# Both feed-forwards: sixteen hidden tiles down by seven half products, two conditioning vectors by TensorE in attention, x added in the later groups

## The chip, the cores and the metric

One core of one Trainium2 chip (trn2). The metric is the device time of one execution in microseconds; the time of a kernel is the median over its runs. The program is written out flat: every instruction is placed once, in a fixed order on each engine, and all loads and stores are issued from one queue, SyncE's, in order.

## The reference, cut to what matters

One trunk layer with two feed-forwards around a token mixer. Context (128 tokens) and latent (1024 tokens) go through the same weights with conditioning vectors of their own. D is 1024, the hidden width of a feed-forward 2816, all in fp32.

```python
def modulate(x, g, shift, scale):
    return rmsnorm(x, g) * (1.0 + scale) + shift

def swiglu(h, w1, w3, w2):
    return (jax.nn.silu(h @ w1) * (h @ w3)) @ w2

def trunk_layer(x, mod, cache, lb, norm_g, ffn1, ffn2, mixer_w):
    m = [mod[:, i][:, None, :] for i in range(N_MOD)]
    x = x + 0.5 * m[2] * swiglu(modulate(x, norm_g[0], m[0], m[1]), *ffn1)
    mix, ctx = token_mixer(modulate(x, norm_g[1], m[3], m[4]), cache, lb, *mixer_w)
    x = x + m[5] * mix
    x = x + 0.5 * m[8] * swiglu(modulate(x, norm_g[2], m[6], m[7]), *ffn2)
    return x, ctx
...
        mod_p = (jax.nn.silu(c_ctx) @ w_ada[l] + b_ada[l]).reshape(1, N_MOD, D_MODEL)
        mod_s = (jax.nn.silu(c) @ w_ada[l] + b_ada[l]).reshape(c.shape[0], N_MOD, D_MODEL)
```

## The kernel before, in words

**Layout.** All 1152 tokens are worked on together, with the features on the partitions: x is eight tiles (KT) of 128 features by 1152 tokens, the hidden layer 22 tiles. Each fp32 operand is split into a high and a low half in fp32r, and a product takes three matmuls: high by high, high by low, low by high. ScalarE makes the high half by a cast, VectorE or GpSimd the low half by a subtraction.

**Stages on TensorE, in order:** the start (conditioning vectors 0 and 1, first norm); the first feed-forward's hidden half (to about 552 us of the profile); its down projection (to 834); the mixer's recurrence and its projections (to about 1560); attention, eight heads with eight steps t of 128 queries each; merge and output projection; the second feed-forward's hidden half (2200 to 2593); its down projection; the final norm.

**Hidden half (`ffn_fast`).** The first PLAIN tiles (4 in the first feed-forward, 3 in the second) are plain products. The others are made by seven half products each: a Strassen-like scheme over two halves of the inner dimension and two of the tokens. The tokens are cut into four quarters of 288, paired (3, 0) and (1, 2). One line, L1746, does these matmuls, with weights from `fast_ops` (cast L1720, low half L1721). Up to six weights are prepared ahead.

**Down projection, the plain form.** `down_group` takes two hidden tiles at a time and forms their product with w2 for eight rows of x and three chunks of 384 tokens: matmuls L473, L474, L475, three per product. VectorE then adds product times gate to x (L502). The first feed-forward did all 22 tiles this way, the last pair and the next norm in `down_last`.

**Down projection, the product form.** The second feed-forward did 16 of its tiles in eight pairs: `down_fast` walks three GROUPS, (first tile, number of pairs) = (3, 2), (7, 3), (13, 3), and in each group four sweeps (m = 0 to 3). A sweep makes the two rows m and m + 4 of x by seven products in the order 1, 6, 7, 5, 2, 4, 3, each for two pairs of quarters (`down_sweep`, L1939, 288 columns). Its parts:

- `pair_sums` (L1783 to L1786, VectorE) forms sums of two hidden tiles in the hidden half; they go to `xd` in DRAM.
- `down_xs` loads them again (`xr`, L1899) and splits them: cast on ScalarE (L1909), low half (L1910) on VectorE for the second pair of a group, else on GpSimd. The next group's are split in the last sweep of a group.
- `pair_weights` (L1807 to L1810, GpSimd) forms the sums of w2 for the first two groups in the hidden half: 5 pairs by 4 m = 20 pieces, stored as `wsum`. The last group's sums are formed on the spot (L1878, GpSimd) in `down_ops`, which also splits all weights (L1883 ScalarE, L1884 VectorE), one product at a time.
- VectorE folds the results: product times gate into x (L1926, in up to two segments where latent and context tokens meet), and products 1 and 6 into a sum `su` (L1942 ScalarE, L1944 VectorE).
- x itself is loaded (`load_x`) under the last hidden tile, two rows at a time (L2056), before the first group.

**Conditioning vectors.** There are nine, m = 0 to 8. `ada_pe` makes 0 and 1 at the start on TensorE: the weights' rows stream against silu(c) of 32 columns, four matmuls side by side on the columns of the array (L263), then a copy and two transposes. `ada_sum` makes the others on VectorE, by products with an accumulated sum (L318): 2 to 5 in the first feed-forward's hidden half, 6 and 7 under its down projection (as `bg`), 8 in the second's hidden half.

**Buffers that matter.** 27 tiles "tt" of 128 x 1152, eight "wide", half and quarter sizes ("half", "hf"); PSUM banks up (3), dn (3), st, ps1 for the feed-forwards and mx (2) among those of attention. A load is issued only when its tile has come free.

## Time and profile before

| | us |
|---|---|
| median of 3 runs (2877.96 to 2881.16) | 2878.12 |
| profiled execution, its own time | 2878.52 |
| its span | 2876.7 |
| TensorE busy in it | 2780.8 |
| start, 0 to 148: TensorE busy | 123.67 of 148 |
| first hidden half, 148 to 552 | 402.37 of 404 |
| first down projection, 552 to 840 | 282.17 of 288 |
| recurrence and projections, 840 to 1560 | 702.28 of 720 |
| attention, 1560 to 1890 | 321.11 of 330 |
| merge, output, next norm, 1890 to 2200 | 293.85 of 310 |
| second hidden half, 2200 to 2593 | 393.00 of 393 |
| its three groups, 2593 to 2784 | 181.72 of 191 |
| last tiles and final norm, 2784 to 2877 | 80.62 of 93 |

The mean granted clock is 0.99. "Busy" is the time in which at least one instruction of an engine ran; matmuls overlap each other, so the pace of a stage is read from its length and its count of matmuls, and not from the mean duration of one (L1939: mean 297 ns). A bracket behind a timeline row, such as `[2.08 <-DVE x L1926]`, is the idle time before it and what ended it.

### The profile page before, as it was taken

What the parts mean: (1) busy time and instruction counts of PE and PEld (TensorE: products, weight loads), DVE (VectorE), ACT (ScalarE), POOL (GpSimd) and SP (SyncE); (2) the same over time, 40 slices, a digit from 0 to 9 for tenths busy, and PEclk for the clock granted to TensorE, in tenths of its full rate; (3) what the DMA queues carried; (4) which work ended last, traced back from release to release, by engine and by line L of the source; (5) the groups of instructions that cost most, each with busy time, mean ns of one, the idle gap of its engine ahead of it and who ended that gap; (6) DMA issues with size and microseconds to landing.
All of it is one profiled execution on the core that took longest, in us unless ns stands there. A gap on an engine that the chain in (4) does not pass through costs nothing. (4 is left out here: it accounts for less than half of the span.)

```text
span 2876.7 us, 55574 instructions
## 1 busy us (share of the span) xinstructions
PE 2780.8 (97%) x21138; PEld 2642.9 (92%) x21138; DVE 2023.5 (70%) x4433; ACT 1324.6 (46%) x2714; POOL 962.9 (33%) x997
## 2 busy tenths in 40 slices
PE   6999999999999999999999999989999999999998
PEld 5999999999999999988998778779989999999997
DVE  7687777577778777877356777756665666568775
ACT  6433323321166676766535787730552322234332
POOL 0132232354222122222144454442442443323450
PEclk9999999999999999999999999999999999999999
DMA  6643333663121111112512001262553443358421
GB/s 238 212 146 124 126 123 115 225 208 109 62 81 55 50 57 37 57 47 68 173 56 75 18 17 30 76 217 91 181 159 108 146 158 127 100 164 264 131 88 66
DMA packets 215147, 329.59 MB, mean 115 GB/s; under 512 B 23712, under 2 KB 138976, under 8 KB 214880
## 3 DMA queue, kind: packets, MB, share of 16 engines
q1 hardware_dynamic: 214880, 326.04, 34.7%
q8 instruction: 167, 2.74, 0.4%
q14 instruction: 100, 0.82, 0.1%
HBM read 243.56 MB, written 82.40 MB: 113 GB/s over the span
## 5 line engine op out<-in xcount | busy, mean ns | idle before, releaser
L1746 PE MATMUL b<-xo,wo 128*128 128x288 f32 x3552 | 482.0, 295 | 0.0
L1746 PEld LDWEIGHTS b<-xo,wo 128*128 128x128 f32 x3552 | 474.3, 188 | 0.0
L1746 PE MATMUL b<-bh,wo 128*128 128x288 f32 x1776 | 365.1, 295 | 1.6 <-ACT et L1756 1.6
L473 PE MATMUL mm<-xh,wh 128*128 128x384 f32 (+1 forms) x1008 | 352.3, 350 | 10.2 <-DVE sg L750 5.6
L474 PE MATMUL mm<-xl,wh 128*128 128x384 f32 (+1 forms) x1008 | 342.4, 340 | 0.0
L475 PE MATMUL mm<-xh,wl 128*128 128x384 f32 (+1 forms) x1008 | 341.9, 339 | 0.0
L1746 PEld LDWEIGHTS b<-bh,wo 128*128 128x128 f32 x1776 | 288.6, 188 | 1.9 <-ACT et L1756 1.8
L502 DVE SCALAR_TENSOR_TENSOR x<-dn,modt,x 128x256 f32<-128x256 f32 (+4 forms) x472 | 225.7, 499 | 87.8 <-PE dn L475 86.5
L1746 PE MATMUL b<-bl,wo 128*128 128x288 f32 x888 | 261.4, 294 | 0.0
L473 PEld LDWEIGHTS mm<-xh,wh 128*128 128x128 f32 (+1 forms) x1008 | 190.0, 188 | 19.9 <-DVE sg L750 7.4
L1720 ACT CAST wo<-raw 128x512 fp32r<-128x512 f32 x185 | 114.8, 621 | 183.7 <-issue 79.5
L474 PEld LDWEIGHTS mm<-xl,wh 128*128 128x128 f32 (+1 forms) x1008 | 189.7, 188 | 2.3 <-issue 0.7
L1939 PE MATMUL d<-xd,wd 128*128 128x288 f32 x1344 | 182.0, 297 | 9.3 <-DVE x L1926 7.8
L475 PEld LDWEIGHTS mm<-xh,wl 128*128 128x128 f32 (+1 forms) x1008 | 189.6, 188 | 1.0
L1939 PEld LDWEIGHTS d<-xd,wd 128*128 128x128 f32 x1344 | 180.1, 190 | 11.1 <-ACT xd L1909 4.0
L1721 DVE TENSOR_TENSOR wo<-raw,wo 128x512 fp32r<-128x512 f32 x185 | 127.8, 692 | 66.6 <-ACT wo L1720 64.2
L318 DVE SCALAR_TENSOR_TENSOR junk<-wada,cb 128x512 bf16<-128x512 f32 x224 | 163.3, 729 | 12.8 <-DMA wada<-in_w_aT 11.9
L1461 POOL TENSOR_TENSOR ehl<-e,ehl 128x512 fp32r<-128x512 f32 x93 | 121.5, 1311 | 142.4 <-ACT ehl L1459 80.6
L1746 PEld LDWEIGHTS b<-bl,wo 128*128 128x128 f32 x888 | 167.0, 188 | 0.0
L247 POOL TENSOR_TENSOR wl<-raw,wh 128x1024 fp32r<-128x1024 f32 (+3 forms) x51 | 101.8, 1996 | 170.3 <-ACT wh L246 113.2
L1721 DVE TENSOR_TENSOR wo<-ws,wo 128x512 fp32r<-128x512 f32 x74 | 71.6, 967 | 112.4 <-ACT wo L1720 112.2
L1720 ACT CAST wo<-ws 128x512 fp32r<-128x512 f32 x74 | 45.6, 617 | 223.2 <-POOL ws L1716 223.1
(438 smaller groups left out, 7176.1 us busy)
## 6 DMA issues: line engine op xcount, KB each, us to landing
raw<-in_w SPq DMA_DIRECT2D x148, 256.0 KB, 3.4
wada<-in_w_aT SPq DMA_DIRECT2D x112, 256.0 KB, 3.2
raw<-in_w SPq DMA_DIRECT2D x42, 512.0 KB, 3.7
raw<-in_w_in SPq DMA_DIRECT2D x41, 512.0 KB, 3.4
xr<-xd SPq DMA_DIRECT2D x56, 288.0 KB, 4.2
hr<-hs SPq DMA_DIRECT2D x26, 576.0 KB, 5.8
hb<-hd SPq DMA_DIRECT2D x44, 288.0 KB, 3.4
hs<-et SPq DMA_DIRECT2D x84, 144.0 KB, 2.2
```

Source lines behind the costliest of these rows:

```text
L247: pin((eng or self.nc.gpsimd).tensor_sub(wl, raw, wh))
L318: nc.vector.scalar_tensor_tensor(junk, ws[n % 2], 1.0, cs[s], ALU.mult, ALU.mult, accum_out=o)
L473: pin(nc.tensor.matmul(ps, wh, xh, start=start and i == 0, stop=False))
L474: pin(nc.tensor.matmul(ps, wh, xl, start=False, stop=False))
L475: pin(nc.tensor.matmul(ps, wl, xh, start=False, stop=stop and i == n - 1))
L502: nc.vector.scalar_tensor_tensor(self.x[m][:, a:b], ps[:, a - lo : b - lo], self.modt[:, gm, m, s : s + 1], self.x[m][:, a:b], ALU.mult, A ...
L1461: eng.tensor_sub(el, e, eh)
L1720: nc.scalar.copy(wh, src[i])
L1721: nc.vector.tensor_sub(wl, src[i], wh)
L1746: nc.tensor.matmul(ps, w[:, k], x[:, k, :QW], start=first, stop=last, skip_group_check=home != i)
L1939: nc.tensor.matmul(ps, w[:, k], xv, start=start, stop=stop, skip_group_check=home != i)
```

## The change

Both feed-forwards now take sixteen hidden tiles, the ones right behind the plain tiles, down by the seven half products, in groups of 2, 3 and 3 pairs; the six others stay plain. `pair_sums` and `pair_weights` run in both hidden halves. `pair_weights` also stores the sums for the last group's m = 0, so there are 5 x 4 + 3 = 23 pieces.

x isn't loaded before the groups. In group 0 the first product to reach a piece of x writes it as product times gate, VectorE for products 7 and 3, ScalarE for 2 and 4. In groups 1 and 2 each sweep loads one row of the old x and adds it after the sweep's fourth product, in two VectorE operations of 576 columns.

Vectors 6 and 7 are made in attention by `ada_fill`: from the second head on, in steps t = 3 and 7, it alternates between loading two rows of weights and eight matmuls on them (four column groups by two rows), with the partial sums added on VectorE and two transposes at the end. The mixer's constants are made in parts during group 1.

```diff
-GROUPS = (3, 2), (7, 3), (13, 3)
+GROUPS = (0, 2), (4, 3), (10, 3)
+PAIRED = 16
...
+    def ada_fill(self):
+
+        nc, a = self.nc, self.a
+        for m in (6, 7):
+            acc = self.fp.tile([P, 256], F32, tag="ada", bufs=1, name="adar")
+            for k in range(0, KT, 2):
+                w = [self.tt(F32, "wada")[:, :D] for _ in range(2)]
+                for i in range(2):
+                    nc.sync.dma_start(w[i], a["w_ada"][(k + i) * P : (k + i + 1) * P, m * D : (m + 1) * D])
+                yield
+                ps = self.pp.tile([P, 256], F32, tag="mx", bufs=2, name="adap")
+                for i in range(2):
+                    for g in range(4):
+                        v = slice(32 * g, 32 * g + 32)
+                        nc.tensor.matmul(
+                            ps[v, :],
+                            self.sc[:, k + i, :],
+                            w[i][:, 256 * g : 256 * g + 256],
...
+                if k:
+                    nc.vector.tensor_add(acc, ps, acc)
+                else:
+                    nc.vector.tensor_copy(acc, ps)
+                yield
+            self.ada_turn(m, acc, "mx", 2)
+            yield
...
+                    if h and t in (3, 7):
+                        next(fill, None)
...
-            for m in range(KT // 2):
+            for m in range(KT // 2 if j < n - GROUPS[-1][1] else 1):
...
-            own = g == len(GROUPS) - 1
+            own = g == len(GROUPS) - 1 and m > 0
...
-        def add(mi, q, src):
+        def add(mi, q, src, new=None):
             for lo, hi, s in segs(QUARTERS[q]):
                 xv, v = self.x[mi][:, lo:hi], slice(lo - q * QW, hi - q * QW)
+                if first and new:
+                    if new == "act":
+                        nc.scalar.activation(xv, src[:, v], AF.Identity, scale=self.modt[:, gm, mi, s : s + 1])
+                    else:
+                        nc.vector.tensor_scalar(xv, src[:, v], self.modt[:, gm, mi, s : s + 1], None, ALU.mult)
+                    continue
                 nc.vector.scalar_tensor_tensor(xv, src[:, v], self.modt[:, gm, mi, s : s + 1], xv, ALU.mult, ALU.add)
...
+                if g:
+                    xa.append((4 * g - 4 + m, load_x(4 * g - 4 + m)))
 
                 def after():
                     nonlocal k
+                    if xa and k == 3:
+                        i, t = xa.pop()
+                        for v in range(2):
+                            c = ts(v, 2 * QW)
+                            self.nc.vector.tensor_add(self.x[i][:, c], t[:, c], self.x[i][:, c])
...
-                if n != 3:
+                if n != (3 if l else 6):
                     next(sums, None)
...
-                        self.x[k] = load_x(k)
-                elif f == NF - 1:
...
+                        self.x[k] = self.tt(F32, f"x{k}")
...
-            self.bg = self.ada_sum((6, 7), lambda: self.bank("up", "cb", D // 2), partial(self.tt, F32), self.slim)
...
+        self.down_fast(w2, X, xg, dops, dmade, load_x, load_h, split_h, gm, nxt)
```

TensorE where the first feed-forward goes from its hidden half to its down projection. `b` is a hidden product, `dn` a plain one of the down projection, `d` a half product of it; `hh` and `hl` are the halves of a hidden tile. Before:

```order
L1746 MATMUL b_6131<-bh,wo 128x288
L473 MATMUL dn<-hh,wh 128x384
L474 MATMUL dn<-hl,wh 128x384
L475 MATMUL dn<-hh,wl 128x384
L473 MATMUL dn<-hh,wxh 128x384
L474 MATMUL dn<-hl,wxh 128x384
L475 MATMUL dn<-hh,wxl 128x384
```

And now, at the same place:

```order
L1787 MATMUL b_6545<-bh,wo 128x288
L1987 MATMUL d_6699<-xd,wd 128x288 x6
L1987 MATMUL d_6707<-xd,wd 128x288 x6
L1987 MATMUL d_6720<-xd,wd 128x288 x6
L1987 MATMUL d_6728<-xd,wd 128x288 x6
L1987 MATMUL d_6747<-xd,wd 128x288 x6
L1987 MATMUL d_6755<-xd,wd 128x288 x6
L1987 MATMUL d_6766<-xd,wd 128x288 x6
L1987 MATMUL d_6774<-xd,wd 128x288 x6
```

The pair of plain tiles that stood first is gone; at once the eight products of the first sweep come, each of six matmuls of 288 columns.

TensorE in the second head of attention, at step t = 7 (`mtr` are transposes of row maxima, `po` the products with the values, `sps` the scores that come next). Before:

```order
L475 MATMUL qps<-qnh_17389,wl 128x384
L1418 MATMUL mtr<-ident,m_18845 1x128 x4
L1428 MATMUL po<-ehl,V 128x512
L1429 MATMUL po<-ehl,V 128x512
L1430 MATMUL po<-ehl,V 128x512
L1452 MATMUL sps<-qh_17836,kth_17721 128x512
L1453 MATMUL sps<-qh_17836,ktl_17722 128x512
L1454 MATMUL sps<-ql_17837,kth_17721 128x512
```

And now:

```order
L511 MATMUL qps<-qnh_18197,wl 128x384
L1459 MATMUL mtr<-ident,m_19658 1x128 x4
L1469 MATMUL po<-ehl,V 128x512
L1470 MATMUL po<-ehl,V 128x512
L1471 MATMUL po<-ehl,V 128x512
L306 MATMUL adap<-wada,sc 32x256 x8
L1493 MATMUL sps<-qh_18644,kth_18529 128x512
L1494 MATMUL sps<-qh_18644,ktl_18530 128x512
L1495 MATMUL sps<-ql_18645,kth_18529 128x512
```

Eight matmuls of vector 6 (`adap`) stand between the last `po` and the first `sps`.

VectorE in the second feed-forward's group 0, third sweep, which makes rows 2 and 6 of x (`d7`, `d5` and so on are PSUM banks of the products, `modt` the gate, `wd` a weight's low half, `xd` that of a sum of hidden tiles). Before:

```order
L1926 SCALAR_TENSOR_TENSOR x6_30109<-d7_30500,modt_92,x6_30109 128x288
L1926 SCALAR_TENSOR_TENSOR x6_30109<-d7_30508,modt_92,x6_30109 128x288
L1884 TENSOR_TENSOR wd_30516<-raw_30338,wd_30516 128x256
L1926 SCALAR_TENSOR_TENSOR x6_30109<-d5_30519,modt_92,x6_30109 128x288
L1926 SCALAR_TENSOR_TENSOR x6_30109<-d5_30527,modt_92,x6_30109 128x288
L1884 TENSOR_TENSOR wd_30535<-raw_30338,wd_30535 128x256
L1926 SCALAR_TENSOR_TENSOR x2_30107<-d1_30452,modt_92,x2_30107 128x160
L1926 SCALAR_TENSOR_TENSOR x2_30107<-d1_30452,modt_92,x2_30107 128x128
L1926 SCALAR_TENSOR_TENSOR x2_30107<-d1_30460,modt_92,x2_30107 128x288
L1884 TENSOR_TENSOR wd_30553<-wq_30405,wd_30553 128x256
```

And now:

```order
L1972 TENSOR_SCALAR x6_31071<-d7_31459,modt_92 128x288
L1972 TENSOR_SCALAR x6_31071<-d7_31467,modt_92 128x288
L1926 TENSOR_TENSOR wd_31475<-raw_31297,wd_31475 128x256
L1974 SCALAR_TENSOR_TENSOR x6_31071<-d5_31478,modt_92,x6_31071 128x288
L1974 SCALAR_TENSOR_TENSOR x6_31071<-d5_31486,modt_92,x6_31071 128x288
L1926 TENSOR_TENSOR wd_31494<-raw_31297,wd_31494 128x256
L1926 TENSOR_TENSOR wd_31512<-wq_31364,wd_31512 128x256
L1952 TENSOR_TENSOR xd_31578<-xr_31403,xd_31578 128x576
L1972 TENSOR_SCALAR x2_31070<-d5_31478,modt_92 128x288
```

Products 7 now write x without reading it, and the additions into `x2` that came from product 2 (`d1`) have left this queue. The additions of the old x stand in the sweeps of the next groups; in group 1's first sweep:

```order
L1974 SCALAR_TENSOR_TENSOR x4_30837<-d7_31850,modt_92,x4_30837 128x288
L1974 SCALAR_TENSOR_TENSOR x4_30837<-d7_31861,modt_92,x4_30837 128x288
L1926 TENSOR_TENSOR wd_31872<-raw_31604,wd_31872 128x384
L1974 SCALAR_TENSOR_TENSOR x4_30837<-d5_31875,modt_92,x4_30837 128x288
L2035 TENSOR_TENSOR x0_30836<-x0_31788,x0_30836 128x576
L1974 SCALAR_TENSOR_TENSOR x4_30837<-d5_31886,modt_92,x4_30837 128x288
L1926 TENSOR_TENSOR wd_31897<-raw_31604,wd_31897 128x384
L2035 TENSOR_TENSOR x0_30836<-x0_31788,x0_30836 128x576
```

Two operations of 576 columns take the loaded row `x0` into the row of x, between the folds of products 7 and 5 and the weights' low halves.

102 lines of the change are left out of this document (44 added, 58 removed).

## The prediction

> **What bounds the kernel now.** I read the head of the page first, then the busy time of each engine by stage, then what TensorE waited for, and last the timeline around its longest waits.
>
> ```profile
> span 2876.7 us, 55574 instructions
> PE 2780.8 (97%) x21138; PEld 2642.9 (92%) x21138; DVE 2023.5 (70%) x4433; ACT 1324.6 (46%) x2714; POOL 962.9 (33%) x997
> PEclk9999999999999999999999999999999999999999
> ```
>
> TensorE is busy 97% of the span and the clock row of the page stands at 9 throughout, so a change is worth what it does to TensorE's stream of matmuls, and work of another engine counts only where it makes that stream stop.
>
> ```profile
> core 0: us, PE busy (x) PEld busy (x) DVE busy (x) ACT busy (x) POOL busy (x), PEclk, DMA share, GB/s
> 560.00:780.00 220.00, 220.00 (x1255) 219.99 (x1254) 171.51 (x414) 41.13 (x40) 96.25 (x39) 1.00 0.42 143
> 2200.00:2593.00 393.00, 393.00 (x2975) 392.98 (x2974) 252.97 (x501) 117.32 (x243) 146.24 (x210) 1.00 0.44 142
> 2593.00:2784.00 191.00, 181.72 (x1346) 179.90 (x1345) 157.11 (x308) 77.15 (x144) 82.73 (x54) 0.99 0.54 170
> ...
> 148.00:552.00 404.00, 402.37 (x3038) 402.15 (x3037) 290.61 (x648) 126.91 (x246) 128.91 (x146) 1.00 0.41 131
> ```
>
> The rows give the pace of a matmul where nothing stops it. Between 560 and 780 us, in the first feed-forward's down projection, 1255 matmuls of 384 columns fill 220.00 us: 0.1753 us each. Between 2200 and 2593, 2975 matmuls of 288 columns fill 393.00 us: 0.1321 each. The second feed-forward's three groups of products (2593 to 2784) hold 1344 matmuls of 288 columns, which at that pace take 177.5 us; they took 191.0. So **13.5 us** of stalls lie there, and they are the best witness for what the first feed-forward will look like. The last row is the first feed-forward before its down projection, where VectorE is busy 290.61 of 404 us.
>
> ```profile
> 1600.00:1800.00 200.00, 198.28 (x954) 159.53 (x954) 148.53 (x280) 155.34 (x298) 96.97 (x82) 1.00 0.08 21
> ```
>
> In attention's middle heads TensorE is busy 198.28 of 200 us: what is added to its stream there is paid in full.
>
> **Part 1, the first feed-forward's down projection.** Sixteen tiles leave the plain form: 16 tiles x 8 rows x 3 chunks x 3 matmuls = 1152 of 384 columns, 1152 x 0.1753 = 201.9 us. In come 4 rows x 7 products x 2 pairs of quarters x 8 pairs of tiles x 3 = 1344 of 288 columns, 1344 x 0.1321 = 177.5 us. Without stalls that is **-24.4 us**. The six tiles left plain cost the same in both.
>
> ```profile
> PE dn L475 <- POOL wl L247: 1.0, 1, 1.0
> PE dn L473 <- DVE x L502: 0.4, 1, 0.4
> ```
>
> These two waits are all that the plain form lost in this stretch, 1.4 us, both where tiles change over; such change-overs stay, so I keep them. What comes in is the stall of the product form, S, which I take from the second feed-forward.
>
> ```profile
> 2637.40 3.60 PE L1939 MATMUL d<-xd,wd 128*128 128x288 f32 x24 [2.08 <-DVE x L1926]
> 2644.78 1.61 PE L1939 MATMUL d<-xd,wd 128*128 128x288 f32 x9 [3.79 <-DVE x L1926]
> ...
> 2724.38 2.63 PE L1939 MATMUL d<-xd,wd 128*128 128x288 f32 x18 [1.44 <-DVE su L1944]
> ...
> 2718.82 3.15 POOL L1910 TENSOR_TENSOR xd<-xr,xd 128x576 fp32r<-128x576 f32 x2
> 2721.93 1.52 POOL L1878 TENSOR_TENSOR wr<-wr,ws 128x384 f32<-128x384 f32 x1
> ...
> 2645.90:2649.30 3.40, 3.40 (x16) 3.40 (x15) 3.40 (x6) 1.80 (x3) 2.86 (x2) 0.50 0.84 254
> ```
>
> The first two rows are the change from group 0 to group 1: TensorE stood 2.08 and 3.79 us until VectorE had folded earlier products. Right behind it the granted clock was 0.50 for 3.4 us (16 matmuls where the next 3.4 us hold twice as many), which costs 1.7 us: 7.6 us in all. The third is in the first sweep of the last group: 1.44 us, and there GpSimd worked a weight sum (L1878) between two splits of `xd` (L1910), so the weight came late. The rest of the 13.5 us are stops under 1 us each.
>
> **Part 2, what the change does to S,** in both feed-forwards alike.
>
> ```profile
> L1926 DVE SCALAR_TENSOR_TENSOR x<-d,modt,x 128x288 f32<-128x288 f32 x114 | 56.3, 510 | 14.0 <-PE d L1939 12.9
> L1910 DVE TENSOR_TENSOR xd<-xr,xd 128x576 fp32r<-128x576 f32 x16 | 18.6, 1165 | 3.8 <-ACT xd L1909 3.7
> L1926 DVE SCALAR_TENSOR_TENSOR x<-d,modt,x 128x160 f32<-128x160 f32 x28 | 10.5, 377 | 1.4 <-PE d L1939 0.7
> L1926 DVE SCALAR_TENSOR_TENSOR x<-d,modt,x 128x128 f32<-128x128 f32 x28 | 9.5, 340 | 0.0
> ...
> L1942 ACT COPY su<-d 128x288 f32<-128x288 f32 x8 | 3.0, 400 | 1.3 <-PE d L1939 1.3
> ...
> 2593.00:2637.90 44.90, 42.45 (x318) 41.86 (x316) 35.71 (x79) 21.27 (x50) 11.71 (x8) 1.00 0.81 265
> 2637.90:2714.00 76.10, 72.31 (x533) 71.97 (x532) 61.43 (x108) 29.18 (x54) 31.95 (x22) 0.98 0.51 151
> 2714.00:2784.00 70.00, 66.96 (x500) 66.07 (x499) 59.97 (x123) 26.70 (x43) 39.07 (x26) 1.00 0.41 129
> ...
> SPq L1848 <- DMA x<-xs: 2.4, 1, 2.4
> SPq L1840 <- DMA x<-xs: 2.1, 2, 1.1
> SPq L1637 <- DMA x<-xs: 2.1, 2, 1.1
> SPq L1853 <- DMA x<-xs: 0.7, 1, 0.7
> ```
>
> (a) The last group's first sweep takes stored sums, so four GpSimd operations and their four waits on loads go: I take 2.5 us of stalls out, the 1.44 us above and about as much of the small ones near it; at least 0, at most 4. Its price, three more pairs' first sums, is made in the hidden half before (part 4).
> (b) In group 0, products 2 and 4 are written by ScalarE: per sweep six pieces of 288, 160 and 128 columns, twice 510 + 377 + 340 = 2.45 us, 9.8 us in four sweeps, leave VectorE, which was busy 35.71 of 44.90 us there. ScalarE, at 21.27 of 44.90, gets them; its nearest row, a copy of 288 columns from PSUM, took 0.400 us, so about 9 us: it stays below 31 of 45, but its queue also holds the weight and `xd` casts on which the change of group hangs. VectorE's remaining writes in group 0 lose their second operand. No row shows a `tensor_scalar` of this shape; between half of 510 ns and 510 ns, I take 510 by the nearest row, the addition it replaces.
> A sentence on the page "VectorE: DVE Perf Modes" of the Trainium skill, under "Why PSUM operands drop a tier", bears on this: an fp32 operand in PSUM keeps VectorE at one element per cycle, so dropping the second operand buys nothing. By it those 16 writes per feed-forward of about 0.5 us stay as dear; without it they would save some 4 us of VectorE's time in group 0, none of it on TensorE by itself. No run here shows it yet.
> (c) SyncE waited 2.4 + 2.1 + 2.1 + 0.7 = 7.3 us for loads of `x` just as group 0 began, with the loads of `xd` queued behind. Those loads move into groups 1 and 2, one per sweep, so group 1's `xd` can start earlier. With (b) I take 2 us off the 7.6 us of the change of group; bounds: 2 us more (ScalarE's longer queue) and 6 us less.
> (d) The adds come back later as 16 operations of 576 columns on VectorE per feed-forward. The row for such a size is L1910's, 1.165 us in the mean: 16 x 1.165 = 18.6 us onto groups 1 and 2, where VectorE is busy 61.43 of 76.10 and 59.97 of 70.00 us. That leaves 6 us of 146: the mean load fits, the bursts at the end of group 1, where `xd` splits stand in the same queue, do not. Behind each add stand the fold of a product (its PSUM bank) and the next weight's low half. I charge 1 us at the change from group 1 to 2 and 0.25 in each of the eight sweeps: 3 us; bounds 0 and 12.
> (e) The load's own wait. An add comes after four products of its sweep, 4 x 18 x 0.1321 = 9.5 us after it starts.
>
> ```profile
> x<-xs SPq DMA_DIRECT2D x8, 576.0 KB, 7.6
> ```
>
> A load of `x` took 7.6 us where eight went out together; singly I expect it in time, cost 0, and price the other case below.
>
> So S = 13.5 - 2.5 - 2 + 3 = 12, less what VectorE gains when GpSimd's sums no longer run beside it in one sweep; I take **S = 10 to 12, 10.5**. First feed-forward: -24.4 + 10.5 = -13.9. Second: 10.5 - 13.5 = **-3.0**.
>
> **Part 3, attention.** 16 rows of weights, each four matmuls of 32 columns of the array, enter TensorE's queue in eight pieces of eight; then two transposes per vector.
>
> ```profile
> 51.77 0.29 PE L475 MATMUL ps<-bh,wl 128*128 128x288 f32 x1
> 51.99 1.07 PE L263 MATMUL adap<-wada,sc 128*32 128x256 f32 x16
> 52.99 0.40 PE L473 MATMUL ps<-bh,wh 128*128 128x288 f32 x1
> 53.23 0.29 PE L474 MATMUL ps<-bl,wh 128*128 128x288 f32 x1
> ...
> 1629.22 0.39 PE L1428 MATMUL po<-ehl,V 128*128 128x512 f32 x1
> 1629.45 0.60 PE L1418 MATMUL mtr<-ident,m 128*1 128x128 f32 x4
> 1629.80 0.47 PE L1429 MATMUL po<-ehl,V 128*128 128x512 f32 x1
> 1630.12 0.39 PE L1430 MATMUL po<-ehl,V 128*128 128x512 f32 x1
> ```
>
> The first rows are the same piece where it stands now, in the start: sixteen records (two passes of each matmul), 1.07 us. Without it the matmul at 53.23 would follow that at 51.77 after two paces, at 52.03; so a piece costs 1.20 us, eight cost 9.6. Four transposes between `po` matmuls (1629.22 to 1630.12, 0.90 us where two paces of 0.23 would be 0.46) cost 0.44 us, so the new four cost 0.4 to 0.6. Sum **+10.1 us**, hidden by nothing, since TensorE stood 1.7 us in those 200. Bounds: 8 (some falls into stops of the later heads) and 13 (waits on a load or a PSUM bank shared with the row maxima). The 64 products on VectorE that it replaces (L318 under the first feed-forward's groups) lay beside a full TensorE, so their removal is worth 0 by itself.
> By the Trainium skill, "TensorE: Matmul & The Clock Gate", Part 3 on packing, column tiles overlap within a pass and a pass lasts one matmul plus about 4 ns per further tile: four passes of 0.39 us make about 1.6 us a piece, 12.5 us in all and a total some 3 us higher (an estimate from that page). The rows above overlap the passes too (1.07 us), and I go by the rows.
>
> **Part 4, the first feed-forward's hidden half.** It now makes pair sums and weight sums.
>
> ```profile
> L1786 DVE TENSOR_TENSOR hp<-et 128x288 f32<-128x288 f32 x16 | 7.3, 455 | 0.3
> ...
> L1810 POOL TENSOR_TENSOR wq<-wq 128x128 f32<-128x128 f32 x17 | 11.2, 656 | 0.0
> ```
>
> Pair sums: 64 operations x 0.455 = 29.1 us on VectorE, 290.61 + 29.1 = 320 of 404 us. Weight sums: 23 pieces x 4 x about 0.63 = 58 us on GpSimd, at 128.91 of 404. The second feed-forward carries both with VectorE at 252.97 of 393 and no stop of TensorE. Here VectorE has the vectors' products besides. Weights are cast up to six products ahead, so a burst has some 3.2 us per product (24 x 0.1321) to drain: I take 0.6 us; bounds 0 and 12.
>
> **The sum.** -24.4 + 10.5 + 0.6 - 3.0 + 10.1 = **-6.2 us**. The profiled execution had a span of 2876.7 and a time of 2878.5, 1.8 outside; the median of the runs is 2878.1. From the median: 2871.9, rounded to **2872**. Own range with S from 7 to 14 and attention from 8 to 12: first -16.8 to -9.8, second -6.5 to +0.5, attention +8 to +12: 2863 to 2881.
>
> **Rivals.**
> *The product form runs clean.* With SyncE free of `x` and GpSimd of four sums, the change of group passes without a stop over 1 us and without the half clock: S = 4 each. -20.4 - 9.5 + 10.1 + 0.6 = -19.2: 2859. For it: the second feed-forward's hidden half runs the same splits with no stop. Against: ahead of group 1 stand 14 splits on GpSimd of about 1.6 us (two took 3.15 above), against a sweep of 84 matmuls, 11 us.
> *VectorE fills up in groups 1 and 2.* A third of the 18.6 us shows, S = 16 to 17: -8.0 + 3.0 + 10.1 + 0.6 = +5.7: 2884. For it: 6 us of slack in 146. Against: the stops of a microsecond and more sit at the changes of group, and within the sweeps a VectorE busy 61.43 of 76.10 us costs little.
> *A late `x` holds VectorE (slower).* Place: the first add of a sweep, at the head of VectorE's queue, waiting for a transfer which SyncE issues only when a tile comes free and earlier loads in its queue have gone. It decides from the point where the load is issued 2 us after its sweep began (9.5 - 7.6). If half of the 16 are 3 us late, 24 us are added: -6.2 + 24 = +18: 2896. Against: one load per sweep has the transfer engines at a share of 0.51 and 0.41.
> *The first feed-forward's hidden half stops.* Eight pairs whose sums (8 x 0.455 = 3.6 us, more than a product's 3.2) hold the next eviction 1.5 us: +12: 2884.
> That the change does not do what it says I leave out: the new order shows all of it.
>
> **How the numbers follow.** Forecast 0.50 (of it 0.36 beyond -0.2%, 0.14 within); clean 0.16, faster; VectorE full 0.16 (0.08 within, 0.08 slower); late `x` 0.10, slower; hidden half 0.08 (0.05 within, 0.03 slower). 0.2% is 5.8 us, about what a measurement of this kernel tells from no change. Together: faster 0.52, same 0.27, slower 0.21. The range leaves out most of late `x` and the far end of clean: 2858 to 2886.
>
> **What would show it.** Right: in the first feed-forward's groups 1344 matmuls in 185 to 192 us; a stop of some microseconds at the change from group 0 to 1 in both, and none from the weight sums in the last group's first sweep; eight pieces of about 1.1 us in attention. Wrong: TensorE waiting for an `x` that waits for a transfer; stops before the down projection; attention longer by under 6 or over 14 us; or groups without stops.

## The result, and the profile after

The changed kernel is slower: 2901.11 us median of 6 runs (2896.81 to 2905.77) against 2878.04 (2874.03 to 2882.57, 6 runs), a ratio of 1.0075, interval 1.0063 to 1.0086. Forecast were 2872 us and a range of 2858 to 2886. The head of its page (span, busy times):

```profile
span 2899.6 us, 57126 instructions
PE 2773.9 (96%) x21462; PEld 2625.6 (91%) x21462; DVE 2064.7 (71%) x4420; ACT 1372.4 (47%) x2876; POOL 1013.4 (35%) x1114
```

TensorE has less to do (2773.9 us where it was 2780.8) and stands longer (126 where it was 96). The next view is the table by stretches, which I cut at the first and last matmul of a stage. Of the changed kernel: first hidden half, first groups, the six plain tiles, second groups.

```profile
core 0: us, PE busy (x) PEld busy (x) DVE busy (x) ACT busy (x) POOL busy (x), PEclk, DMA share, GB/s
151.20:580.20 429.00, 409.47 (x3025) 406.80 (x3024) 320.84 (x715) 119.77 (x256) 179.09 (x238) 0.98 0.55 169
580.30:769.30 189.00, 182.12 (x1345) 179.93 (x1344) 162.17 (x308) 81.00 (x165) 75.26 (x48) 0.99 0.57 173
769.40:846.50 77.10, 77.10 (x437) 76.57 (x436) 51.18 (x105) 34.37 (x62) 27.22 (x18) 1.00 0.30 107
2616.70:2807.10 190.40, 180.99 (x1347) 178.50 (x1346) 163.65 (x306) 82.43 (x166) 75.17 (x49) 1.00 0.58 181
```

And the first hidden half of the kernel before, cut in the same way:

```profile
150.20:552.50 402.30, 400.67 (x3025) 400.45 (x3024) 289.08 (x646) 125.64 (x244) 126.71 (x144) 1.00 0.41 132
```

The first hidden half is the news. For the same 3025 matmuls TensorE stood 19.5 us where it had stood 1.6, and was busy 8.8 us longer, at a mean clock of 0.98: slow matmuls behind the stops. VectorE's and GpSimd's busy time don't show it, 320.84 and 179.09 of 429. By such cuts the two profiled executions (spans 2876.7 and 2899.6) differ so:

| stage, us | before | after | difference | forecast |
|---|---|---|---|---|
| first hidden half | 402.3 | 429.0 | +26.7 | +0.6 |
| first down projection (groups 189.1, rest 77.2) | 281.4 | 266.3 | -15.1 | -13.9 |
| attention, first score to last value product | 326.3 | 333.5 | +7.2 | +10.1 |
| second hidden half | 422.0 | 424.1 | +2.1 | 0 |
| second groups | 191.1 | 190.4 | -0.7 | -3.0 |
| all else | 1253.6 | 1256.3 | +2.7 | 0 |
| sum | 2876.7 | 2899.6 | +22.9 | -6.2 |

One line is off by far more than the rest together. What waited for what in that half (engine and line, what it waited for, total us, times, longest):

```profile
PE b L1787 <- ACT et L1797: 11.8, 8, 2.9
PE b L1787 <- DVE et L1795: 7.7, 3, 3.3
...
ACT wo L1761 <- POOL ws L1757: 143.2, 17, 14.3
...
DVE junk L354 <- DMA wada<-in_w_aT: 38.2, 12, 5.9
...
POOL wq L1849 <- DMA wq<-in_w: 103.7, 18, 12.6
...
SPq L1854 <- POOL wq L1851: 43.5, 17, 4.4
```

TensorE's 11 waits are for folds: product 2's on ScalarE, product 5's on VectorE. In the same stretch ScalarE stood 143.2 us with its casts for GpSimd's sums of the hidden weights (`ws`), VectorE 38.2 for the vectors' weights, GpSimd 103.7 for the loads of the weight sums, SyncE 43.5 in front of their stores. Such totals don't say which wait held a fold. The timeline around the longest stop does (SyncE's issues, then GpSimd, ScalarE, VectorE, TensorE):

```profile
327.04 0.81 SPq L1846 DMA_DIRECT2D wq<-in_w  x2
331.82 0.33 SPq L1854 DMA_DIRECT2D wsum<-wq  x1
332.69 0.33 SPq L1855 DMA_DIRECT2D wsum<-wq  x1
333.07 0.91 SPq L1739 DMA_DIRECT2D raw<-in_w  x2
334.08 0.38 SPq L335 DMA_DIRECT2D wada<-in_w_aT  x1
...
329.44 0.97 POOL L1849 TENSOR_TENSOR wq<-wq 128x128 f32<-128x128 f32 x1 [2.34 <-DMA wq<-in_w]
331.34 0.46 POOL L1851 TENSOR_TENSOR wq<-wq 128x128 f32<-128x128 f32 x1
331.76 0.91 POOL L1852 TENSOR_TENSOR wq<-wq 128x128 f32<-128x128 f32 x1
336.65 1.43 POOL L1757 TENSOR_TENSOR ws<-raw 128x256 f32<-128x256 f32 x2 [3.98 <-DMA raw<-in_w]
338.04 1.41 POOL L1757 TENSOR_TENSOR ws<-ws,raw 128x256 f32<-128x256 f32 x2
...
339.48 0.62 ACT L1761 CAST wo<-ws 128x512 fp32r<-128x512 f32 x1 [9.60 <-POOL ws L1757]
...
334.11 0.45 DVE L1793 TENSOR_TENSOR et<-b,et 128x288 f32<-128x288 f32 x1
338.89 1.11 DVE L354 SCALAR_TENSOR_TENSOR junk<-wada,cb 128x512 bf16<-128x512 f32 x1 [4.33 <-DMA wada<-in_w_aT]
340.13 1.00 DVE L1762 TENSOR_TENSOR wo<-ws,wo 128x512 fp32r<-128x512 f32 x1
341.06 0.45 DVE L1795 TENSOR_TENSOR et<-b,et 128x288 f32<-128x288 f32 x1
...
335.04 3.34 PE L1787 MATMUL b<-xo,wo 128*128 128x288 f32 x24
341.65 0.37 PE L1787 MATMUL b<-bh,wo 128*128 128x288 f32 x1 [3.27 <-DVE et L1795]
```

Read it backwards. TensorE stood 3.27 us for VectorE's L1795 (341.06). Two operations stand ahead of it in VectorE's queue: the vectors' product L354, which VectorE reached at 334.56 and could not start for 4.33 us, since its weights (`wada`) were issued at 334.08 only, and L1762, the low half of a hidden weight. L354 was through at 340.00. L1762 needs ScalarE's cast of the same weight, which ended at 340.10; it started at 340.13. So the cast is what held the fold: with `wada` there in time, L1762 could have started only 0.03 us earlier. The cast had waited 9.60 us for GpSimd's sum `ws` (L1757), and GpSimd 3.98 us for its load, `raw`. SyncE issued `raw` at 333.07, because it stood from 327.85 to 331.82 in front of L1854, the store of a weight sum that GpSimd was still forming (L1851 ended at 331.80, L1852 at 332.67); `wada` stood there too. GpSimd in turn was late because its own loads, issued at 327.04, had just come. So in this stop it is one loop through one queue: a store that waits for an engine makes every load behind it late, those of the engine itself among them.

All eleven stops end in this way: the fold comes right behind the cast or the low half of a `ws` weight that was late. TensorE never waited for the weight itself, which is prepared several products ahead of its use; the fold stood behind it in the queue. In ten of the eleven GpSimd had just stood for `raw` (0.65 to 6.09 us). In six, 14.6 of the 19.5 us, `raw` was the next load behind the stores of a weight sum. The longest stop on ScalarE:

```profile
435.46 0.62 ACT L1761 CAST wo<-ws 128x512 fp32r<-128x512 f32 x1 [9.30 <-POOL ws L1757]
...
437.35 0.70 ACT L1797 ACTIVATE et<-b 128x288 f32<-128x288 f32 x2
...
437.85 0.37 PE L1787 MATMUL b<-bh,wo 128*128 128x288 f32 x1 [2.94 <-ACT et L1797]
```

The Trainium skill, "PSUM — Partial Sum Buffer", section "Engine vs sequencer instructions", says that the queues of ScalarE, VectorE and GpSimd are strictly first in, first out. The trace agrees: the folds L1795 and L1797 came only after operations on weights that they have nothing to do with, and that were late by the casts' waits of 9.60 and 9.30 us.

### The profile page after: what moved, and what is told of

It reads as the page before. It is cut to its first block, busy times and chain, and to the rows that moved or that the text cites. A ratio compares the mean times of both kernels' runs of the same rounds, so it can differ in the third digit from the quotient of the medians.

```text
span 2899.6 us, 57126 instructions
## 1 busy us (share of the span) xinstructions
PE 2773.9 (96%) x21462; PEld 2625.6 (91%) x21462; DVE 2064.7 (71%) x4420; ACT 1372.4 (47%) x2876; POOL 1013.4 (35%) x1114
## 5 line engine op out<-in xcount | busy, mean ns | idle before, releaser
L1787 PE MATMUL b<-bh,wo 128*128 128x288 f32 x1776 | 373.3, 299 | 19.5 <-ACT et L1797 11.8
L1987 PE MATMUL d<-xd,wd 128*128 128x288 f32 x2688 | 363.5, 296 | 16.3 <-DVE x L1974 14.3
L1987 PEld LDWEIGHTS d<-xd,wd 128*128 128x128 f32 x2688 | 358.6, 189 | 21.0 <-ACT wd L1925 10.2
L509 PE MATMUL mm<-xh,wh 128*128 128x384 f32 (+1 forms) x1008 | 351.8, 349 | 11.4 <-DVE sg L788 5.7
L509 PEld LDWEIGHTS mm<-xh,wh 128*128 128x128 f32 (+1 forms) x1008 | 189.1, 188 | 21.3 <-DVE sg L788 7.5
L510 PEld LDWEIGHTS mm<-xl,wh 128*128 128x128 f32 (+1 forms) x1008 | 189.3, 188 | 2.3 <-issue 0.7
L511 PEld LDWEIGHTS mm<-xh,wl 128*128 128x128 f32 (+1 forms) x1008 | 189.0, 187 | 0.9
L1952 POOL TENSOR_TENSOR xd<-xr,xd 128x576 fp32r<-128x576 f32 x70 | 118.4, 1717 | 173.5 <-ACT xd L1951 129.1
L1762 DVE TENSOR_TENSOR wo<-raw,wo 128x512 fp32r<-128x512 f32 x185 | 129.7, 702 | 37.8 <-ACT wo L1761 35.2
L1762 DVE TENSOR_TENSOR wo<-ws,wo 128x512 fp32r<-128x512 f32 x74 | 71.8, 970 | 114.0 <-ACT wo L1761 113.1
L354 DVE SCALAR_TENSOR_TENSOR junk<-wada,cb 128x512 bf16<-128x512 f32 x160 | 120.5, 753 | 44.1 <-DMA wada<-in_w_aT 43.4
L509 PE MATMUL ps<-bh,wh 128*128 128x288 f32 (+1 forms) x448 | 136.3, 305 | 5.6 <-DVE sl L1717 4.0
```

Source lines behind the costliest of these rows:

```text
L354: nc.vector.scalar_tensor_tensor(junk, ws[n % 2], 1.0, cs[s], ALU.mult, ALU.mult, accum_out=o)
L509: pin(nc.tensor.matmul(ps, wh, xh, start=start and i == 0, stop=False))
L510: pin(nc.tensor.matmul(ps, wh, xl, start=False, stop=False))
L511: pin(nc.tensor.matmul(ps, wl, xh, start=False, stop=stop and i == n - 1))
L1762: nc.vector.tensor_sub(wl, src[i], wh)
L1787: nc.tensor.matmul(ps, w[:, k], x[:, k, :QW], start=first, stop=last, skip_group_check=home != i)
```

## The experiments

All stage lengths are from one profiled execution each, medians and intervals from the timed runs (each beside the kernel before on the same chip). "First half" is the first hidden half. The profiled execution of a_gpst took 2901.23 us and that of a_deep 2887.67, so their stages lie above and below what the medians go with. Runs that leave a stage as it is in the changed kernel show how far single executions differ: the second groups took 188.7 to 190.4 us in seven of them (after, a_own, a_noada, d_nosum, a_rawtt, x_dve, x_dve2), attention 333.4 to 335.3 in sixteen (all but before, b_fill, v_own and v_q).

| run | first half | first groups | attention | second groups | median | ratio to before, interval |
|---|---|---|---|---|---|---|
| before | 402.3 | - | 326.3 | 191.1 | 2878.04 | |
| after | 429.0 | 189.1 | 333.5 | 190.4 | 2901.11 | 1.0075, 1.0063 to 1.0086 |
| a_own | 402.7 | 199.4 | 334.8 | 190.2 | 2884.43 | 1.0011, 1.0001 to 1.0020 |
| a_noada | 407.8 | 189.6 | 334.6 | 188.7 | 2880.48 | 1.0001, 0.9990 to 1.0012 |
| d_nosum | 407.1 | 190.0 | 334.7 | 189.3 | 2877.97 | 0.9990, 0.9980 to 1.0000 |
| a_late | 435.7 | 188.2 | 333.4 | 190.2 | 2907.58 | 1.0091, 1.0076 to 1.0106 |
| a_gap | 435.3 | 189.3 | 333.7 | 188.6 | 2907.85 | 1.0097, 1.0082 to 1.0112 |
| a_rawtt | 428.2 | 190.8 | 334.4 | 189.0 | 2898.03 | 1.0062, 1.0048 to 1.0075 |
| a_gpst | 424.2 | 190.5 | 334.8 | 189.6 | 2893.84 | 1.0036, 1.0023 to 1.0048 |
| a_deep | 419.4 | 189.6 | 334.7 | 189.5 | 2892.61 | 1.0040, 1.0025 to 1.0055 |
| x_dve | 427.2 | 188.9 | 334.5 | 189.2 | 2897.41 | 1.0058, 1.0043 to 1.0074 |
| w_g | 413.7 | 190.5 | 334.7 | 188.3 | 2885.91 | 1.0020, 1.0010 to 1.0030 |
| w_rawtt | 421.1 | 192.6 | 334.7 | 190.5 | 2891.96 | 1.0042, 1.0030 to 1.0055 |
| x_dve2 | 411.3 | 192.0 | 335.3 | 188.9 | 2879.24 | 0.9996, 0.9987 to 1.0005 |
| x_dve3 | 406.4 | 192.2 | 334.5 | 189.3 | 2880.04 | 0.9994, 0.9985 to 1.0004 |
| b_fill | 404.1 | - | 334.6 | 191.6 | 2890.65 | 1.0031, 1.0020 to 1.0042 |
| a_early | 428.2 | 190.3 | 334.7 | 190.8 | 2903.72 | 1.0070, 1.0055 to 1.0085 |
| a_gadd | 429.9 | 196.6 | 334.9 | 197.8 | 2930.43 | 1.0160, 1.0142 to 1.0179 |
| v_own | 401.9 | 199.2 | 323.2 | 189.3 | 2894.86 | 1.0044, 1.0030 to 1.0058 |
| v_q | 415.4 | 193.6 | 324.6 | 188.7 | 2899.07 | 1.0064, 1.0051 to 1.0076 |

### Which added work stops the first half

**a_own**: weight sums on the spot.

```diff
-            own = g == len(GROUPS) - 1 and m > 0
+            own = self.plain == 4 or g == len(GROUPS) - 1 and m > 0
...
-        sums = self.pair_weights(w2)
+        sums = self.pair_weights(w2) if l else iter(())
```

> The changed kernel, but the first feed-forward forms its weight sums on the spot in all three groups (GpSimd, as the last group does), and nothing of them in its hidden half. Theory Q (SyncE's queue stands in front of the store of a weight sum until GpSimd has made it; the loads of the vectors' weights behind it come late; VectorE waits for them in order, with the folds behind): the hidden half falls from 429 to 403-406 us, the groups rise from 189 to 192-197, in all 2879-2885. Rival D (VectorE is too full with the 64 pair sums, which stay): the hidden half stays at 420 or more, in all 2896 or more. Rival G (GpSimd has too much and makes the hidden weights' sums late): as Q.

The half is back at 402.7 us with all pair sums in it; the groups pay 10.3, more than expected. Its row of the same stretch, 151 to 552, with VectorE busier than in the kernel before:

```profile
151.00:552.00 401.00, 399.01 (x3013) 398.78 (x3012) 315.58 (x714) 123.72 (x252) 126.12 (x148) 1.00 0.47 147
```

So all of the 26.3 us go with the weight sums, and the pair sums, the mechanism of my rival for this half, cost nothing by themselves. Weight sums without pair sums were not run.

**a_noada** forms one vector there and fills the other three from it.

```diff
-        ada = self.ada_sum((8,) if l else (2, 3, 4, 5), None, partial(self.tt, F32), self.slim)
+        ada = self.ada_sum((8,) if l else (2,), None, partial(self.tt, F32), self.slim)
```

> The changed kernel without the products of vectors 3, 4 and 5 in the first feed-forward (48 of 64 units, with their loads): they are filled from vector 2's sums. This leaves the first feed-forward's hidden half with 16 units, as the second's has. Theory V (SyncE's queue has room for the weight sums or for four vectors, not for both): the hidden half falls to 403-408. If the weight sums alone stop TensorE in this half, whatever the vectors do: 415 or more, as with the vectors' loads made early (419.4).

407.8: with 16 units as in the second feed-forward, the weight sums cost about 5 us. It takes both, the sums and four vectors, to lose the 26.7; so the second hidden half, which has 16 units, was no witness for this one. Why these 5 us remain, where the second hidden half has no stop, isn't shown.

**d_nosum** takes GpSimd's part out: it stores what it loaded, and the sums are left out.

```diff
+                if self.plain != 4:
+                    nc.gpsimd.tensor_tensor(s1, a21, a22, ALU.add)
...
```

> The changed kernel without GpSimd's four operations per weight sum in the first feed-forward: what was loaded is stored in their place, so loads, stores and their order in SyncE's queue stay. If GpSimd's order stops TensorE (sums of the down weights standing for their loads ahead of the hidden weights' sums): the hidden half falls from 429 to 403-410. If SyncE's queue does it by itself: 418 or more.

407.1: with all loads and stores but no sum to wait for, 22 of the 26.7 us are gone, so it isn't the traffic of the transfers. The run takes out two waits at once, GpSimd's for the loads of the sums and SyncE's for the sums, and doesn't tell them apart.

### Which wait it is

Five edits ease one wait each.

**a_late** and **a_gap** move one step of `pair_weights` by a product; in the first the store:

```diff
                 nc.gpsimd.tensor_tensor(a12, a12, s2, ALU.subtract)
                 yield
+                yield
                 nc.sync.dma_start(self.wsum[j][:, m, 0:2], a[:, P:].rearrange("p (k d) -> p k d", k=2))
...
-                if n != (3 if l else 6):
-                    next(sums, None)
+                next(sums, None)
```

> The changed kernel, the store of each weight sum one product later in SyncE's queue (3.2 us), with the steps of the weight sums taken at all seven products of a tile. Theory Q: SyncE's waits for the sums (43.5 us) fall below 15, VectorE's waits for the vectors' weights (38.2) below 15, the hidden half falls to 405-415. D and G: the hidden half stays within 425-432, since nobody's work changes.

in the second the sums (with the steps at all seven products here too):

```diff
                 yield
                 yield
+                yield
                 nc.gpsimd.tensor_tensor(s1, a21, a22, ALU.add)
```

> The changed kernel with GpSimd's weight sums one product later behind their loads (three products, 9.6 us, where it was two), steps at all seven products; stores from SyncE as before. If the root is GpSimd's order (it stands 103.7 us in the first hidden half for the loads of the sums, and the hidden weights' sums and SyncE's stores stand behind it): that wait falls below 50 us and the hidden half from 429 to 410-418. If the loads come late by as much as they are given (SyncE's queue is what is late): the wait stays above 80 and the hidden half at 425 or more.

Neither came as expected: 435.7 and 435.3. SyncE's wait for the sums was 51.3 and 50.2 us, GpSimd's for the loads 84.8 in the second: room for one member of the loop did not make the loads come in time.

**a_rawtt** puts the hidden weights into large tiles:

```diff
+            else:
+                t = raws[i] = self.tt(F32, "raw")[:, :D].rearrange("p (v n) -> p v n", v=2)
```

> The changed kernel, the first feed-forward's hidden weights loaded into the large tiles, of which some are free, so that SyncE's queue doesn't stand at such a load until VectorE has read the weight before (44.9 us in the hidden half). If that wait is what makes the sums' loads late: GpSimd's wait for them falls from 103.7 to under 60 and the hidden half from 429 to 405-416. If not: 422 or more.

No change clear of noise (428.2); GpSimd's wait for the loads stayed at 103.3 us.

**a_gpst** and **a_deep**:

```diff
-                nc.sync.dma_start(self.wsum[j][:, m, 0:2], a[:, P:].rearrange("p (k d) -> p k d", k=2))
+                nc.gpsimd.dma_start(self.wsum[j][:, m, 0:2], a[:, P:].rearrange("p (k d) -> p k d", k=2))
```

> The changed kernel, the stores of the weight sums issued by GpSimd, right behind its own sums, and no longer by SyncE, in both feed-forwards. Theory Q: with no wait for GpSimd in SyncE's queue (43.5 us) the loads behind it come in time; the first feed-forward's hidden half falls from 429 to 404-410 us, in all 2876-2884. Rival W (GpSimd itself is the late one: it stands in order for its own loads, 103.7 us, and the sums for the hidden weights stand behind): the hidden half stays at 420 or more. If issuing the stores takes GpSimd's time, it gets worse than 429.

```diff
-            if n + 1 < len(units):
-                load(n + 1)
+            if n + 2 < len(units):
+                load(n + 2)
```

> The changed kernel, the vectors' weights loaded two units ahead into four buffers where it was one ahead into two. Theory Q: VectorE's waits for them (38.2 us) fall below 10 and the hidden half to 405-412, since only the lateness of these loads holds the folds. D: no change (425-432). G: stops that come through the hidden weights (ScalarE's cast waiting for GpSimd's sums) stay, 420-430.

Each gives some: by the ratios to the kernel before about 11 of the 22 us go with the stores and 10 with the early loads. With the early loads VectorE's waits for `wada` are gone (0.2 us), and TensorE still stops eleven times, 14.4 us, each time behind a late `ws` weight, as rival G says; what the early loads gain comes by another way than these waits, and it isn't shown which. With the stores in GpSimd's queue SyncE stands 34.4 us for stores to end, where it was 11.4, and GpSimd's own order takes over. Of the ten stops that end behind a `ws` weight, six have its sum right behind a weight sum and GpSimd's issue of its two stores, as in the longest, 3.68 us at 480.13:

```profile
473.82 0.56 POOL L1854 DMA_DIRECT2D wsum<-wq  x1
474.37 0.54 POOL L1855 DMA_DIRECT2D wsum<-wq  x1
474.93 1.43 POOL L1757 TENSOR_TENSOR ws<-raw 128x256 f32<-128x256 f32 x2
```

`raw` had been issued at 469.79, and GpSimd did not stand for it. So a `ws` is late for two reasons: its load comes late through SyncE's queue, and it stands behind the weight sums in GpSimd's. Neither Q nor W alone accounts for the loss, and how it divides between them isn't shown.

**x_dve** has VectorE form the sums.

```diff
-                nc.gpsimd.tensor_tensor(s1, a21, a22, ALU.add)
+                (nc.gpsimd if self.plain == 3 else nc.vector).tensor_tensor(s1, a21, a22, ALU.add)
...
```

> The changed kernel, the first feed-forward's weight sums formed by VectorE, all loads and stores as they were. If GpSimd's order is the cause: the hidden half falls from 429 to 404-413, with 92 more short operations on VectorE, in all 2876-2886. If the sums stop the engine that has them wherever they stand (VectorE standing for their loads, folds behind): 420 or more, in all 2892 or more.

427.2: my reading of the run without sums, that GpSimd's order alone is the cause, falls. Whichever engine forms them, SyncE stands for it (25.9 and 12.1 us in front of L1854 for VectorE here), `raw` comes late, and nine of the eleven stops, 15.9 of 17.0 us, still end behind a `ws` weight. And a_gpst, where SyncE doesn't stand for the sums, keeps half of the loss (1.0036 for 1.0075).

**Together.** w_g joins a_gpst, a_deep, a_gap's gap and five small buffers; w_rawtt adds a_rawtt to it; x_dve2 is x_dve with the early loads and the five buffers; x_dve3 adds a_late's step.

> All of it together, vectors 6 and 7 on TensorE in attention as in the changed kernel: weight sums three products behind their loads, their stores from GpSimd's queue at once, five small buffers, the first feed-forward's vectors' weights two units ahead. If GpSimd's order was what remained in the run with the other three (415.4): the hidden half 403-408 and in all 2874-2882, level with the kernel before. If not: 412 or more and 2884 or more.

> The same on top of the kernel with all the other easings (413.7 in the hidden half): if the hidden weight's load is what remains, 403-407 and in all 2870-2879, faster than the kernel before by 0.05 to 0.4 per cent; if GpSimd's order remains, 410 or more and 2882 or more.

> The same with the vectors' weights two units ahead and five small buffers in the first feed-forward: if late loads are what is left on VectorE, the hidden half 402-406 and in all 2872-2879, faster than the kernel before by 0.05 to 0.3 per cent; if VectorE is then too full, no better than the run beside it.

> The version with the sums on VectorE, the vectors' weights two units ahead and five small buffers, now with the stores of the weight sums one product later (steps at all seven products of a tile, both feed-forwards). If the stores' wait in SyncE's queue holds what is left: SyncE's wait for the sums falls from 35.9 to under 10, the first hidden half from 411.3 to 403-407, in all 2870-2876, faster than the kernel before by 0.15 to 0.35 per cent. If not: the half stays at 409 or more and the whole within 0.1 per cent of the run before it (2879).

413.7, 421.1, 411.3 and 406.4: several easings do what none does alone, and one more can undo some of it. Every stop left in these halves ends behind a `ws` weight: 10.1, 16.3, 6.3 and 3.0 us. In x_dve3 the half came out as expected, but the wait that was to vanish did not: SyncE's waits there,

```profile
SPq L1856 <- DVE wq L1853: 23.8, 10, 5.2
SPq L1856 <- DVE wq L1852: 14.4, 10, 2.5
```

still sum to 38.2 us. So why its half is 4.9 us shorter than x_dve2's isn't shown. Untested: an order in which the folds stand ahead of the casts. Both are level with the kernel before; no version beat it.

### The other parts

**b_fill**, the kernel before with `ada_fill` and no `bg`:

```diff
-            self.bg = self.ada_sum((6, 7), lambda: self.bank("up", "cb", D // 2), partial(self.tt, F32), self.slim)
+            self.bg = iter(())
...
+                    if h and t in (3, 7):
+                        next(fill, None)
```

> The kernel before with one part of the change alone: vectors 6 and 7 by TensorE in attention, none under the first feed-forward's down projection. If the prediction's price was right: attention (first score to last product with the values) 326.3 to 336 us, the down projection stays at 281.4, in all 2888. If what the changed kernel showed (333.5) is this part: 2885. If taking 64 products off VectorE under the down projection frees TensorE there: under 2883.

+8.3 us in attention; the down projection stays at 281.3: 64 products off VectorE freed nothing there. A piece in attention, in the changed kernel:

```profile
1629.64 0.39 PE L1471 MATMUL po<-ehl,V 128*128 128x512 f32 x1
1629.96 1.07 PE L306 MATMUL adap<-wada,sc 128*32 128x256 f32 x16
1630.96 0.50 PE L1493 MATMUL sps<-qh,kth 97*128 97x512 f32 x1
```

From the last `po` to the first `sps` 1.32 us where a pace is 0.23: 1.09 a piece. The prediction's estimate from the Trainium skill (1.6, from "TensorE: Matmul & The Clock Gate", Part 3) is too high here; the row decides.

**a_early** undoes the late x in the second feed-forward:

```diff
-                        self.x[k] = self.tt(F32, f"x{k}")
+                        self.x[k] = load_x(k) if l else self.tt(F32, f"x{k}")
...
-                if g:
+                if g and nxt == 1:
                     xa.append((4 * g - 4 + m, load_x(4 * g - 4 + m)))
...
-                if first and new:
+                if first and new and self.plain == 4:
```

> The changed kernel with one part undone in the second feed-forward: x is loaded under the last hidden tile and every fold adds into it on VectorE, as before; the stored sums for the last group's first sweep stay. By the prediction's terms (2 us more at the first change of group, 3 us of additions gone) its groups go from 190.4 to 189.5; if the additions fill VectorE: 185-187; if the load of x at the start of group 0 was the larger cost: 192 or more.

190.8 against 190.4, less than single executions of this stage differ: the terms for the late x, ScalarE's share and the additions cancel, as far as one execution can tell.

**a_gadd**, the additions on GpSimd:

```diff
-                            self.nc.vector.tensor_add(self.x[i][:, c], t[:, c], self.x[i][:, c])
+                            self.nc.gpsimd.tensor_add(self.x[i][:, c], t[:, c], self.x[i][:, c])
```

> The changed kernel, the additions of the old x (groups 1 and 2, both feed-forwards) on GpSimd, not VectorE. If they make VectorE the bound in those groups (it is busy 63.26 of 68.3 us in the last one): groups 189.1 and 190.4 fall to 183-187 each, in all 2901 to 2891-2896. If GpSimd's splits of the next group's sums come late for it, or the additions wait longer there: 189 or more. If the additions were covered: 188-191.

7 us worse in each set of groups, and 6 more in the plain tiles behind (83.8 against 77.2, 85.9 against 80.3). Its rows in the second groups, and the same operation's on VectorE in the changed kernel:

```profile
L2035 POOL TENSOR_TENSOR x<-x,x 128x576 f32<-128x576 f32 x16 | 24.0, 1522 | 18.4 <-DMA x<-xs 11.0 <-DVE x L1974 7.3
...
L1974 DVE SCALAR_TENSOR_TENSOR x<-d,modt,x 128x160 f32<-128x160 f32 x17 | 6.4, 377 | 10.4 <-POOL x L2035 10.2
```

```profile
L2035 DVE TENSOR_TENSOR x<-x,x 128x576 f32<-128x576 f32 x16 | 14.8, 927 | 4.2 <-DMA x<-xs 4.0
L1972 DVE TENSOR_SCALAR x<-d,modt 128x288 f32<-128x288 f32 x16 | 7.9, 510 | 0.6 <-PE d L1987 0.6
L1974 DVE SCALAR_TENSOR_TENSOR x<-d,modt,x 128x288 f32<-128x288 f32 x92 | 45.6, 510 | 6.7 <-PE d L1987 5.6
```

On GpSimd an addition takes 1522 ns, where VectorE's takes 927, and stands for its load first; VectorE then waits 10.2 us for the sum before it folds on.

**v_own** and **v_q** take vectors 6 and 7 off TensorE again, into the merge (`next(ada, None)` ahead of each gate product), v_own on a_own, v_q on a_gpst, a_deep and five small buffers.

> The changed kernel with the first feed-forward's weight sums on the spot (as in the run that did that alone) and with vectors 6 and 7 off TensorE: by products on VectorE while the branches are merged, one step behind each of its 64 products with a gate. If TensorE's part in attention is pure cost: attention falls from 334.8 to 326-327, the stretch from attention to the second hidden half stays within 3 us of 281.3, since VectorE is busy 169 of 283 us there, in all 2874-2879 beside a kernel before of 2881. If VectorE's waits for the vectors' weights hold the merge: that stretch grows by 8 or more, and nothing is won.

> The changed kernel with the weight sums kept in the hidden half and every wait that was found there eased: their stores from GpSimd's queue, the vectors' weights two units ahead in the first feed-forward, five small buffers instead of three for the sums (so that a load needn't wait for a store's end); vectors 6 and 7 in the merge as in the other run of this pair. If SyncE's order was the cause: the first hidden half falls from 429 to 404-409, the groups stay at 189, in all 2868-2874. If GpSimd's own order (hidden weights' sums behind the down weights' sums) is what remains: 415 or more, in all 2880 or more.

Attention falls to 323.2 and 324.6, but the stretch from there to the second hidden half grows from 281.3 in a_own to 307.7 and 310.6: VectorE had room on the average, not where it folds. TensorE's waits in v_own from 1890 us on (in a_own, `mt` held it 2.1 us and `dn` 4.2):

```profile
PE ups L509 <- DVE mt L1579: 13.4, 12, 1.9
PE dn L509 <- DVE x L538: 7.1, 3, 3.2
PE ups L509 <- DVE mt L1577: 4.5, 3, 1.8
```

## Why the prediction was wrong

**The step that failed** is part 4, the first hidden half at 0.6 us with bounds of 0 and 12; it cost 26.7. I added 29.1 us of pair sums to VectorE's 290.61 and 58 us of weight sums to GpSimd's 128.91 of 404 us and found room, and took the second feed-forward as witness. The busy times came out nearly as added (320.84 and 179.09); the waits were put at nothing. I also counted on weights being cast up to six products ahead. A weight does have that time, but its cast and its low half stand in the queues of ScalarE and VectorE ahead of folds that don't: all eleven stops, 19.5 us, end there. These weights were late because GpSimd's sums for them were, through the order in SyncE's queue, which I read for x at the start of group 0 but not here, and in GpSimd's own. SyncE's holds loads of 64 units of vectors, of the hidden weights and of the sums, with the stores of the sums between. The witness had 16 units, and the price with 16 here is 5 us (407.8); without the weight sums it is nothing (402.7).

**The rival for that half** (+12, 2884) named pair sums that hold an eviction. By themselves they cost nothing; the loss came with the weight sums, which I had put into the same sentence as covered.

**First groups:** S 189.1 - 177.5 = 11.6 us, forecast 10.5. Right in size, not in make-up: the change of group cost 3.8 us (one stop of 2.05, and 1.7 by a clock of 0.69 and 0.81 in the 6.8 us behind it) where 5.6 were kept, and five stops in the last group sum to 4.2 us. That is in part luck. The step from 12 to 10.5, for VectorE without GpSimd's sums beside it, has no row behind it, and no run shows it by itself. The half clock was read a little high: the 3.4 us after it hold 27 matmuls for 16, not twice as many. The six plain tiles took 77.2 us where 281.4 - 201.9 = 79.5 were kept, so the stage gained 15.1 where 13.9 were forecast.

**Second groups:** S 190.4 - 177.5 = 12.9, forecast 10.5; gain 0.7 for 3.0. The stop of the weight sums in the last group's first sweep is gone, and so is the one of 3.79 us at the change of group. Others came: the last view, of the second groups after, has ten waits for VectorE,

```profile
PE d L1987 <- DVE x L1974: 8.5, 9, 2.1
PE d L1987 <- DVE su L1992: 0.9, 1, 0.9
```

none over 2.1 us. VectorE is fuller, 163.65 of 190.40 where it was 157.11 of 191.00. So "VectorE fills up" is half true, and by the run that undid the late x it is worth less than one execution can tell. The addition took 927 ns in the mean for my 1165, the `tensor_scalar` 510, as its neighbour with two operands; by the rule of the Trainium skill cited in the prediction ("VectorE: DVE Perf Modes") it should buy nothing, and the trace agrees.

**Late x** held VectorE 4.0 us in the second groups (the releaser in the row of L2035 above), not 24: right to give it little.

**Attention:** forecast 10.1; 7.2 in the changed kernel, 8.3 alone, up to 9.0 in the others. The piece cost 1.09 for 1.20.

**The sign** hung on the one term. With 0.6 in place of 26.7 the measured stages sum to -3.2 us, within what a measurement of this kernel tells from no change, and that is where the versions that ease the half came out (ratios 0.9996 and 0.9994). So even without the failure the gain was too high by half: 2.1 us in the second hidden half, 2.3 in the second groups and 2.7 elsewhere were not in the sum, against 4.1 better in attention and the first down projection.

**Open:** how the loss divides between SyncE's queue and GpSimd's, and which wait keeps the last 4 to 11 us of the eased versions. The stops left there still end behind late hidden weights; no single wait ahead of those is shown to be the cause.

## What to carry to other kernels

Before adding a load, a sum and a store to a stage with spare engine time, write down what stands behind each of them in every in-order queue, and what each waits for: a store behind a computation is a wait in the queue that issues everyone's loads. Look too at what stands ahead of an urgent operation in its own queue: a weight that isn't needed for several products held a fold that was needed at once. When reading a stop, follow the wait that ended last; the one beside it (4.33 us for `wada`) held nothing. A stage that carries the same work without a stop is a witness only if it has the same other traffic in that queue. A loop of waits isn't mended by moving one member by a step; count on needing several easings, or take the work out (402.7).

## What the runs showed of the hardware that I had not expected

A stop doesn't always cost clock, and its length doesn't tell. These are the 3.4 us behind stops of 3.27, 2.94, 1.80 and 2.18 us in the changed kernel's first hidden half, with a granted clock of 1.00, 0.69, 0.59 and 1.00:

```profile
341.60:345.00 3.40, 3.35 (x23) 3.19 (x24) 3.37 (x8) 2.26 (x5) 0.12 (x1) 1.00 0.31 87
437.80:441.20 3.40, 3.35 (x18) 3.38 (x19) 3.37 (x10) 1.28 (x3) 0.00 (x0) 0.69 0.27 77
172.20:175.60 3.40, 3.40 (x16) 3.40 (x17) 3.37 (x8) 0.62 (x2) 2.06 (x3) 0.59 0.32 101
292.80:296.20 3.40, 3.33 (x25) 3.33 (x26) 3.37 (x10) 1.30 (x3) 0.00 (x0) 1.00 0.28 84
```
